# A hybrid gated-DeltaNet and dilated-attention block on one core: the key convolution's SiLU held behind the block inverse on ScalarE, and four sigmoids of a projection unit put together

## Chip, cores and metric

The kernel runs on one core of a Trainium2 chip. The metric is the device time of one execution in microseconds (us). TensorE is called PE, VectorE DVE, ScalarE ACT, GpSimd POOL, and SyncE SP; SP issues all of this kernel's DMAs.

## What is computed

One layer: the input x (1024 tokens, 1024 columns) is normalised and projected to 11280 columns; a gated delta rule over 8 heads and a dilated window attention over 12 heads run on parts of the projection; sigmoid gates (`g_a`, `g_b`) merge the two branches; an output projection, a residual and a last norm follow. What the change touches:

```python
qkv = jax.nn.silu(_causal_conv(concat([q_a, k_a, v_a]), conv_w))     # 4 taps per channel
q_a, k_a, v_a = split(qkv)
o_a = _gated_delta_rule(l2norm(q_a), l2norm(k_a), v_a, beta, g)      # chunks of 64 tokens
merged = jax.nn.sigmoid(g_a) * y_a + jax.nn.sigmoid(g_b) * y_b
```

In the delta rule each chunk of 64 tokens solves a unit lower triangular system `m u = rhs`, and a state of 128x128 is handed from chunk to chunk.

## The kernel before

**Projections.** The large products run as units of two blocks of 128 columns each. A unit (`gemm_steps`, L199) has seven products of 12 matmuls with 512 columns each, after a scheme that saves an eighth of the multiplications; each product goes to one of the PSUM banks `p_ga`, `p_gb`, `p_gc`. For each product ACT makes the high part `wh` of a weight tile (L140) and DVE the low part `wl` (L142). ACT copies the two results of bank `p_ga` out (L207 and L219), DVE adds the others (L210, L223 and L131). The third product of a unit (operand A12) writes `p_ga` again, so PE waits there until L207 has read the first.

**The delta rule.** It lies between the projection units. A half head (512 tokens, four blocks of 128) is one round, and there are 16 rounds of nearly equal length. For a round the kernel runs: the convolutions of k, q and v (`conv`: ACT scales by the first weight at L950, DVE adds three taps at L953, ACT applies SiLU at L956); `dn_prep`, which transposes k and q on PE (L1000), squares and sums them on ACT (L1003, each with a read of the accumulator), scales k into `kd`, the decay matrix into `am` and v into `vp` on ACT (all L966), and inverts blocks of 16 on DVE with a chain of small steps (L1051, L1053); `dn_run`, which doubles the inverses from 16 to 32 to 64 to 128 (L1084 to L1127) and then walks the four blocks (L1138 to L1163). The last doubling is: PE product at L1120, ACT copy to `Wv` at L1122, PE product at L1126, ACT copy into `XT` at L1127. These steps belong to different half heads: while one round's inverse is doubled, a later round's k is convolved.

**The gates.** `gate_pair` makes a projection unit whose two blocks are gate columns. Each block has two halves of 512 tokens; when a half is finished, ACT applies the sigmoid in place (L762) and SP stores it to HBM (L763). The results lie in tiles `d4`, of which there are five. Two such units (columns 0 to 511 of `g_b`) follow directly on the first head's q, k, v and z units, where the delta rule begins; the others come at the end of the delta rule.

**What sets the order.** PE runs in the order in which the program is written: every unit is a generator, and tables of positions (`CONV`, `INVERSE`, `LEVELS` and the like) say after which matmul of which unit the next step of each generator is emitted. On ACT, DVE, POOL and SP a scheduler chooses the order when the program is built, from the dependences and its own estimate of the times; `tc.issue_after(i)` adds that an instruction is to stand behind instruction `i` on its engine. `behind(last_kd)` in `conv` is such a rule: the SiLU stands behind the four `kd` instructions last written down. At run time every engine works strictly through its own list. ACT has one set of function tables active; where the next function is not in it, an ACT_TABLE_LOAD stands ahead of it. SiLU and sigmoid lie in different sets, copy and square are in each.

The change touches `gate_pair` (L750 to L765), the list of units (L872), `conv` (L947 to L957), its callers (L974, L977, L979), and L1127.

Of the kernel before, what the change touches and what calls it, by code (L numbers as in the profile page):

```python
# [11 lines left out]
AF = mybir.ActivationFunctionType  # L12
# [19 lines left out]
def hybrid_block(ctx: ExitStack, tc: tile.TileContext, x, norm_w, w_in, conv_w, a_log, dt_bias,  # L32
                 dn_norm_w, w_o_dn, w_o_dil, w_out, final_norm_w, out):
    nc = tc.nc
    V, A, G, T = nc.vector, nc.scalar, nc.gpsimd, nc.tensor
# [8 lines left out]
    def pst(tag, bufs=1):  # L44
        return ps.tile([128, 512], F32, name="p_" + tag, tag=tag, bufs=bufs)
# [9 lines left out]
    def d4():  # L55
        return dp.tile([128, 1028], F32, name="d4", tag="d4")
# [394 lines left out]
    def cw(tap, blk):  # L451
        return colp[:, tap * 24 + blk:tap * 24 + blk + 1]
# [86 lines left out]
    sg_d = {n: [dr.tile([128, S], F32, name=f"s{n}{i}") for i in range(8)] for n in ("a", "b")}  # L539
# [191 lines left out]
    def dn_unit(h, pair, t):  # L731
        def dest(n):
            o = 0 if n == "z" else 3

            def f(hf):
                if n not in t:
                    t[n] = d4()
                    if n != "z":
                        V.memset(t[n][:, 0:3], 0.0)
                return t[n][:, o + hf * 512:o + (hf + 1) * 512], idv  # L740
            return f

        def z_after(hf):
            v = t["z"][:, hf * 512:(hf + 1) * 512]
            A.activation(v, v, AF.Silu)
            nc.sync.dma_start(zsp_d[h][:, hf * 512:(hf + 1) * 512], v)

        return [(OFF[n + "a"] + h * 128, dest(n), z_after if n == "z" else nop) for n in pair]

    def gate_pair(n, i):  # L750
        bl = []
        for e in range(2):
            s = []

            def dest(hf, s=s):
                if not s:
                    s.append(d4())
                return s[0][:, hf * 512:(hf + 1) * 512], idv

            def af(hf, s=s, n=n, j=i + e):  # L760
                v = s[0][:, hf * 512:(hf + 1) * 512]
                A.activation(v, v, AF.Sigmoid)  # L762
                nc.sync.dma_start(sg_d[n][j][:, hf * 512:(hf + 1) * 512], v)  # L763
            bl.append((OFF["g" + n] + (i + e) * 128, dest, af))
        return bl  # L765

# [4 lines left out]
    def merged_at(i, hf):  # L771
        return merged[i // 4][:, hf * 4:hf * 4 + 4, i % 4]
# [34 lines left out]
    def att_head(hh, t):  # L807
        st = ap_.tile([128, 48], F32, name="st", bufs=2)
        nums = []
        return [attention(g, hh, t, st, nums) for g in range(3)] + [merge(hh, st, nums, t)]  # L810
# [51 lines left out]
    gates = [(n, i) for n in "ba" for i in range(0, 8, 2)]  # L862
    att_heads = [{} for _ in range(AH)]
    heads = [{} for _ in range(NH)]
    units = []
# [3 lines left out]
    for h in range(NH):  # L869
        units += [dn_unit(h, "qk", heads[h]), dn_unit(h, "vz", heads[h])]  # L870
        if h == 0:
            units += [gate_pair(*g) for g in gates[:2]]  # L872
    units += [gate_pair(*g) for g in gates[2:GATES]]
    units += [gate_pair(*g) for g in gates[GATES:]]
    units = [(b, w2, hops) for b in units]
    aops = {}
# [31 lines left out]
    for hh in range(AH):  # L908
        g0, g1, g2, m = att_head(hh, att_heads[hh])
# [28 lines left out]
    def full(t):  # L938
        return t[:, :16384].rearrange("c (i j) -> i c j", j=128)


    last_sub, last_wv, last_xt, last_kd = [None], [None], [None], [None]

    def behind(i):
        return tc.issue_after(i[0].ins) if i[0] else nullcontext()

    def conv(dst, u, blk, hf, late):  # L947
        o = hf * 512
        vw = (lambda a: a.rearrange("p (c t) -> p c t", t=128)) if len(dst.shape) == 3 else idv
        A.activation(dst, vw(u[:, o:o + 512]), AF.Copy, scale=cw(0, blk))  # L950
        for tap in range(1, 4):
            with behind(late):
                V.scalar_tensor_tensor(dst, vw(u[:, o + tap:o + tap + 512]), cw(tap, blk), dst, OP.mult, OP.add)  # L953
            if tap == 3:
                with behind(last_kd):
                    A.activation(dst, dst, AF.Silu)  # L956
            yield  # L957

# [12 lines left out]
    def dn_conv(h, hf, t, o):  # L971
        c0 = hf * 4
        qk = o["qk"] = dnp.tile([128, 4, 2, 128], F32, name="qk", bufs=3)
        yield from conv(qk[:, :, 0], t["k"], 8 + h, hf, last_xt)  # L974

    def qv_conv(h, hf, t, o):
        yield from conv(o["qk"][:, :, 1], t["q"], h, hf, last_sub)  # L977
        vT = o["vT"] = dnp.tile([128, 512], F32, name="vT")
        yield from conv(vT, t["v"], 16 + h, hf, last_sub)  # L979

    def dn_prep(h, hf, o):
        c0 = hf * 4
# [80 lines left out]
    def dn_run(h, hf, o, state):  # L1063
        c0 = hf * 4
        qk, am, aq, kd, vp, ce = (o[n] for n in ("qk", "am", "aq", "kd", "vp", "ce"))
        qd = qk[:, :, 1]
        X = dnp.tile([128, 4, 128], F32, name="X")
        XT = dnp.tile([128, 4, 128], F32, name="XT")
        i = nc.sync.dma_start(XT, full(inv_d[hf][1]))
# [11 lines left out]
        def prod64(lhs, rhs):  # L1081
            p = pst("ch", 2)
            for c in range(4):
                T.matmul(p[:, c * 64:(c + 1) * 64], lhs[:, c], rhs[:, c], start=True, stop=True)  # L1084
            return p
# [4 lines left out]
        pxt = prod64(X, Wv)  # L1090
# [8 lines left out]
        for c in range(4):  # L1099
            for i in range(2):  # L1100
                r, q = slice(i * 64, i * 64 + 32), slice(i * 64 + 32, i * 64 + 64)
# [11 lines left out]
        for v, p, q in ((XT, 0, 32), (XT, 64, 96), (X, 32, 0)):  # L1113
            A.activation(v[p:p + 32, :, q:q + 32], px[p:p + 32, :128].rearrange("p (c m) -> p c m", c=4), AF.Copy,
                         scale=-1.0)
# [8 lines left out]
        pxt = pst("ch", 2)  # L1124
        for c in range(4):
            T.matmul(pxt[:64, c * 64:(c + 1) * 64], X[:64, c, :64], W[:, c], start=True, stop=True)  # L1126
        A.activation(XT[:64, :, 64:], pxt[:64, :256].rearrange("p (c m) -> p c m", c=4), AF.Copy, scale=-1.0)  # L1127


        po = pst("o")  # L1130
# [73 lines left out]
    for n in range(2 * NH):  # L1204
        h, hf = n // 2, n % 2
        state = state if hf else [None]
        o = {}
        add_stream(dn_conv(h, hf, heads[h], o), steps(spread(n - 1, CONV, 4)))
        add_stream(qv_conv(h, hf, heads[h], o), steps(spread(n - 1, QV_CONV, 7)))
        add_stream(dn_prep(h, hf, o), steps([n + p for p in PREP] + spread(n, INVERSE, 16)))  # L1210
        add_stream(dn_run(h, hf, o, state), steps([n + LOAD] + spread(n + 1, LEVELS, 7) + spread(n + 1, CHAIN, 12)))
        add_stream(dn_out(h, hf, o), steps([n + 1 + p for p in OUT]))
# [168 lines left out]
    for k in range(4):  # L1381
        t = d4()[:, :S]
# [12 lines left out]
    for i in range(8):  # L1395
# [7 lines left out]
        for hf in range(2):  # L1403
            v, mv = sg[:, hs[hf]], merged_at(i, hf)
# [23 lines left out]
    for i in (0, 2, 4, 6):  # L1428
# [57 lines left out]
        with band(-1) if i == 0 else nullcontext():  # L1486
            gemm_unit(oops, lambda cb, kf, i=i: merged[kf][:, i + cb], 8,
                      lambda cb, hf, y=y: (y[cb][:, hs[hf]], idv), normed, residual if last else None, i == 0, stores, sums=V,
# [29 lines left out]
```

## Time and profile before

| | |
|---|---|
| median of 3 runs | 1437.64 us (1436.38 to 1439.87) |
| the profiled execution | 1437.49 us, of which the span from the first to the last instruction is 1435.8 us |
| mean granted clock of PE | 0.992 |
| busy: PE, DVE, ACT, POOL | 1387.7, 1076.0, 726.0, 438.7 us |
| table loads on ACT | 25 |

A row of a timeline holds the start in us from the span's start, the length in us, the engine, the line, the operation, the tile written and read, and in brackets the idle time before it and the instruction that ended it. Neighbouring rows of one kind are merged (x4). Lengths of PE rows overlap, as matmuls are pipelined.

### The profile page before, as it was taken

The page shows a single profiled execution, that of the slowest core. Times are in us where ns is not written, and L with a number is a line of the kernel's source. Part 1 is how long each engine was busy: PE and PEld are TensorE (multiplying, and loading weights), DVE is VectorE, ACT ScalarE, POOL GpSimd, SP SyncE. Part 2 cuts the span into 40 slices and gives each one's busy share as a digit, 9 for nine tenths or more (in the row PEclk, how much of TensorE's full clock was granted, in tenths as well). Part 3 has the DMA queues.
Part 4 walks back from the last instruction along what each step waited for, and adds up shares of the span by engine and source line. Part 5 has one row for each costly group of instructions (what it writes and reads, how often), then busy time and mean ns, then how long its engine had stood idle before and what let it go on. Part 6 is the DMA issues. An engine that isn't in the chain of part 4 may idle for free.

```text
span 1435.8 us, 22591 instructions
## 1 busy us (share of the span) xinstructions
PE 1387.7 (97%) x7627; PEld 1128.1 (79%) x7627; DVE 1076.0 (75%) x2305; ACT 726.0 (51%) x1830; POOL 438.7 (31%) x411
## 2 busy tenths in 40 slices
PE   7999999999999999899999999999999999999997
PEld 4788888888888888677777777777777777787786
DVE  6865567558558558778888888888887558888976
ACT  5444534534443444756555655656566436424433
POOL 6122232232323223233333333333333122431022
PEclk9999999999999999999999999999999999999999
DMA  6012333242334225533333333333334359669631
GB/s 194 24 50 67 92 101 106 67 120 87 87 83 114 75 58 135 169 84 107 98 107 100 108 113 113 99 99 106 99 107 122 111 159 296 207 219 341 215 117 59
DMA packets 228536, 172.84 MB, mean 120 GB/s; under 512 B 48802, under 2 KB 190531, under 8 KB 228420
## 3 DMA queue, kind: packets, MB, share of 16 engines
q1 hardware_dynamic: 228420, 171.40, 40.3%
q8 instruction: 60, 0.98, 0.3%
q14 instruction: 56, 0.46, 0.1%
HBM read 127.10 MB, written 44.25 MB: 119 GB/s over the span
## 4 chain that ended last, share of the span: by engine, by line
PE 78%; DVE 13%; DMA 3%; ACT 3%; issue 2%; POOL 1%; SPq 0%; POOLq 0%; DVEq 0%; ACTq 0%
PE p_gb L199 24%; PE p_ga L199 17%; PE p_gc L199 16%; DVE qk L953 5%; PE p_o L624 2%; PE p_ch L601 2%; DVE wl L142 2%; PE p_ch L1084 2%; PE p_w L1017 2%; PE p_ch L1147 1%; PE p_w L614 1%; DMA sg<-oA 1%; PE p_ch L1154 1%; PE p_o L1163 1%; PE p_ch L1126 1%
## 5 line engine op out<-in xcount | busy, mean ns | idle before, releaser
L140 ACT ACTIVATE wh<-raw 128x512 fp32r<-128x512 f32 x283 | 177.4, 628 | 276.1 <-PE p_gc L199 102.1
L142 DVE TENSOR_TENSOR wl<-raw,wh 128x512 fp32r<-128x512 f32 x283 | 208.6, 737 | 40.1 <-ACT wh L140 17.2
L174 POOL TENSOR_TENSOR raw<-raw,t 128x512 f32<-128x512 f32 x46 | 68.0, 1478 | 167.6 <-DVE wl L142 159.4
L171 POOL TENSOR_TENSOR raw<-raw,t 128x512 f32<-128x512 f32 x46 | 62.5, 1359 | 181.6 <-DVE wl L142 141.6
L953 DVE SCALAR_TENSOR_TENSOR qk<-d,colp,qk 128x512 f32<-128x512 f32 x96 | 112.1, 1169 | 1.0
L156 POOL TENSOR_TENSOR raw<-raw 128x512 f32<-128x512 f32 x47 | 72.3, 1538 | 106.9 <-DMA raw<-in_w_in_dram 57.3
L131 DVE TENSOR_TENSOR d<-p_gc,d 128x512 f32<-128x512 f32 x86 | 59.3, 690 | 41.6 <-PE p_gc L199 41.6
L199 PE MATMUL p_ga<-A12H,wh 128*128 128x512 f32 x200 | 84.9, 425 | 3.8 <-ACT d L207 3.8
L1144 POOL COPY gate<-rh 128x1 f32<-128x1 f32 x16 | 14.0, 874 | 243.1 <-DVE rh L1140 243.1
L607 ACT ACTIVATE sm<-sm,st 128x128 f32<-128x128 f32 (+1 forms) x96 | 43.1, 449 | 87.1 <-DVE st L605 87.0
L199 PE MATMUL p_gc<-S4H,wh 128*128 128x512 f32 x204 | 81.6, 402 | 1.9 <-DVE d L131 1.9
L199 PE MATMUL p_gb<-A22H,wh 128*128 128x512 f32 x204 | 82.5, 407 | 0.5 <-DVE d L210 0.5
L199 PE MATMUL p_ga<-A12L,wh 128*128 128x512 f32 x200 | 82.1, 411 | 0.0
L199 PE MATMUL p_gb<-A22L,wh 128*128 128x512 f32 x204 | 80.6, 397 | 0.0
L199 PE MATMUL p_gb<-S3H,wh 128*128 128x512 f32 x188 | 78.5, 420 | 1.9 <-DVE d L210 1.9
L199 PE MATMUL p_gc<-S4L,wh 128*128 128x512 f32 x204 | 80.2, 395 | 0.0
L199 PE MATMUL p_ga<-A11H,wh 128*128 128x512 f32 x184 | 79.5, 432 | 0.6 <-DVE gl L519 0.6
L199 PE MATMUL p_gb<-S2H,wh 128*128 128x512 f32 x188 | 79.3, 424 | 0.0
L199 PE MATMUL p_gc<-S1H,wh 128*128 128x512 f32 x188 | 78.7, 420 | 0.0
L199 PE MATMUL p_gb<-S3L,wh 128*128 128x512 f32 x188 | 76.4, 408 | 0.0
L199 PE MATMUL p_gb<-S2L,wh 128*128 128x512 f32 x188 | 76.3, 408 | 0.0
L199 PE MATMUL p_gc<-S1L,wh 128*128 128x512 f32 x188 | 75.6, 404 | 0.0
(591 smaller groups left out, 3938.7 us busy)
## 6 DMA issues: line engine op xcount, KB each, us to landing
raw<-in_w_in_dram SPq DMA_DIRECT2D x176, 256.0 KB, 2.9
wb<-w_d SPq DMA_DIRECT2D x24, 256.0 KB, 3.7
dr<-gcr_d SPq DMA_DIRECT2D x32, 128.0 KB, 3.0
dec<-de SPq DMA_DIRECT2D x32, 128.0 KB, 1.8
decq<-dr SPq DMA_DIRECT2D x32, 128.0 KB, 1.8
zsp<-d SPq DMA_DIRECT2D x16, 256.0 KB, 2.6
sb<-d SPq DMA_DIRECT2D x16, 256.0 KB, 3.3
R<-egcr_d SPq DMA_DIRECT2D x16, 256.0 KB, 3.5
```

Of the source, the lines that this page charges most:

```text
L131: last_add[0] = V.tensor_tensor(dst, vw(banks[bank]), dst, OP.add)
L140: A.activation(wh[:, :kh], v, AF.Copy)
L142: i = eng.tensor_tensor(wl[:, :kh], v, wh[:, :kh].bitcast(F32), OP.subtract)
L156: e.tensor_tensor(b12, b22, b12, OP.subtract)
L171: i = (lead["eng"] if lead else G).tensor_tensor(b11, b22, t2, OP.subtract)
L174: (sums or G).tensor_tensor(b21, b21, t2, OP.subtract)
L199: T.matmul(pt, w[:, k], m, start=new and n == 0, stop=n == len(prods) - 1, skip_group_check=not new)
L601: T.matmul(pk[:, :n], q[:, m * 128:(m + 1) * 128], k[:, (m + 1) * 128 - n:(m + 1) * 128], start=True, stop=True)
L607: last_exp[0] = A.activation(sm[:, :n], sm[:, :n], AF.Exp, scale=-1.0, bias=st[:, c_m:c_m + 1], accum_out=st[:, c_d:c_d + 1])
L624: T.matmul(po[:, j * 128:(j + 1) * 128], vt[:, m + 1 - n // 128 + i], pT[:, i * 128:(i + 1) * 128], start=i == 0, stop=i == n // 128 - 1)
L953: V.scalar_tensor_tensor(dst, vw(u[:, o + tap:o + tap + 512]), cw(tap, blk), dst, OP.mult, OP.add)
L1017: T.matmul(pk[:, j * 256:(j + 1) * 256], qk[:, c, 0], qk[:, c].rearrange("p s t -> p (s t)"), start=True, stop=True)
```

## The change

The SiLU of k is held behind the copy into `XT` that ends the last doubling (`last_inv`, L1127) instead of behind the `kd` instructions; those of q and v are held as before. In the first two gate units the four halves wait for one another: when the last is finished, four sigmoids stand in a row, the last-made half first, each followed by its store. Every other gate unit is as before.

```diff
-    def gate_pair(n, i):
-        bl = []
+    def gate_pair(n, i, together=False):
+        bl, parts = [], []
...
             def af(hf, s=s, n=n, j=i + e):
-                v = s[0][:, hf * 512:(hf + 1) * 512]
-                A.activation(v, v, AF.Sigmoid)
-                nc.sync.dma_start(sg_d[n][j][:, hf * 512:(hf + 1) * 512], v)
+                parts.append((s[0][:, hf * 512:(hf + 1) * 512], sg_d[n][j][:, hf * 512:(hf + 1) * 512]))
+
+                if not together or len(parts) == 4:
+                    first = None
+                    for v, d in parts[::-1]:
+                        with tc.issue_after(first.ins) if first else nullcontext():
+                            i = A.activation(v, v, AF.Sigmoid)
+                        first = first or i
+                        nc.sync.dma_start(d, v)
+                    parts.clear()
...
-            units += [gate_pair(*g) for g in gates[:2]]
+            units += [gate_pair(*g, together=True) for g in gates[:2]]
...
-    def conv(dst, u, blk, hf, late):
+    def conv(dst, u, blk, hf, late, silu):
...
             if tap == 3:
-                with behind(last_kd):
+                with behind(silu):
                     A.activation(dst, dst, AF.Silu)
...
-        yield from conv(qk[:, :, 0], t["k"], 8 + h, hf, last_xt)
+        yield from conv(qk[:, :, 0], t["k"], 8 + h, hf, last_xt, last_inv)
...
-        yield from conv(o["qk"][:, :, 1], t["q"], h, hf, last_sub)
+        yield from conv(o["qk"][:, :, 1], t["q"], h, hf, last_sub, last_kd)
...
-        yield from conv(vT, t["v"], 16 + h, hf, last_sub)
+        yield from conv(vT, t["v"], 16 + h, hf, last_sub, last_kd)
...
-        A.activation(XT[:64, :, 64:], pxt[:64, :256].rearrange("p (c m) -> p c m", c=4), AF.Copy, scale=-1.0)
+        last_inv[0] = A.activation(XT[:64, :, 64:], pxt[:64, :256].rearrange("p (c m) -> p c m", c=4), AF.Copy, scale=-1.0)
```

PE's order is the same instruction for instruction; only ACT's, DVE's, POOL's and SP's lists differ. The number of table loads falls from 25 to 21. From L957 on, the changed kernel's lines are those of before plus seven (L956 is L963, L1122 is L1129); L762 is L767, and L763 is L769.

ACT's list before, in the fourth round (X is the inverse so far, `jk` takes the squares, `qk` is the SiLU of k, `wh` a weight part):

```order
L1114 ACTIVATE XT<-p_ch 32x4x32 x2
L1114 ACTIVATE X<-p_ch 32x4x32
L1003 ACTIVATE jk,ssq<-p_w 128x128 x2
L956 ACTIVATE qk<-qk 128x4x128
L1003 ACTIVATE jk,ssq<-p_w 128x128
L1122 ACTIVATE Wv<-p_ch 64x256
L1003 ACTIVATE jk,ssq<-p_w 128x128
L140 ACTIVATE wh<-raw 128x512
L1127 ACTIVATE XT<-p_ch 64x4x64
L966 ACTIVATE vp<-p_w,sm 128x128 x4
```

The same place in the changed kernel:

```order
L1121 ACTIVATE XT<-p_ch 32x4x32 x2
L1121 ACTIVATE X<-p_ch 32x4x32
L1010 ACTIVATE jk,ssq<-p_w 128x128 x4
L1129 ACTIVATE Wv<-p_ch 64x256
L140 ACTIVATE wh<-raw 128x512
L1134 ACTIVATE XT<-p_ch 64x4x64
L963 ACTIVATE qk<-qk 128x4x128
L973 ACTIVATE vp<-p_w,sm 128x128 x4
```

The SiLU moved from ahead of `Wv` to behind `XT`; all four squares now stand ahead of `Wv`. The same holds in all 13 rounds from the second to the fourteenth; in the first round the SiLU stood ahead of all four squares and moved likewise; the last two rounds have no SiLU of k.

ACT's list before, where the delta rule begins (d_5460 and d_5489 are the two blocks of the first gate unit, d_5698 is the next unit's first block):

```order
L1003 ACTIVATE jk,ssq<-p_w 128x128 x2
L762 ACT_TABLE_LOAD
L762 ACTIVATE d_5460<-d_5460 128x512
L956 ACT_TABLE_LOAD
L956 ACTIVATE vT<-vT 128x512
L1003 ACTIVATE jk,ssq<-p_w 128x128
L762 ACT_TABLE_LOAD
L762 ACTIVATE d_5489<-d_5489 128x512
L1003 ACTIVATE jk,ssq<-p_w 128x128
L966 ACTIVATE kd<-p_w,eglc 128x128 x4
L966 ACTIVATE am<-am,sm 128x128 x4
L207 ACTIVATE d_5698<-p_ga 128x512
```

The same place in the changed kernel:

```order
L1010 ACTIVATE jk,ssq<-p_w 128x128 x2
L973 ACTIVATE kd<-p_w,eglc 128x128 x3
L963 ACTIVATE vT<-vT 128x512
L973 ACTIVATE kd<-p_w,eglc 128x128
L140 ACTIVATE wh<-raw 128x512
L767 ACT_TABLE_LOAD
L767 ACTIVATE d_5489<-d_5489 128x512
L767 ACTIVATE d_5460<-d_5460 128x512
L767 ACTIVATE d_5489<-d_5489 128x512
L767 ACTIVATE d_5460<-d_5460 128x512
L973 ACTIVATE am<-am,sm 128x128 x4
L207 ACTIVATE d_5698<-p_ga 128x512
```

One table load instead of three stands ahead of `am` in this stretch, and four sigmoids instead of two.

DVE's list before at the same place (`ssq` and `sm` are the small steps from the squares to the factor of `am`; L953 on d_5094 are taps of k):

```order
L142 TENSOR_TENSOR wl<-raw,wh 128x512
L953 SCALAR_TENSOR_TENSOR qk<-d_5094,colp,qk 128x4x128 x2
L1010 TENSOR_SCALAR ssq<-ssq 128x4
L1024 TENSOR_TENSOR sm<-sm,beta 128x4
L1025 TENSOR_TENSOR sm<-sm 128x4
L1026 SCALAR_TENSOR_TENSOR sm<-sm,egc 128x4
L210 TENSOR_TENSOR d_5735<-p_gb,d_5698 128x512
```

The same place in the changed kernel (`ssq` stands six rows above the first one shown):

```order
L1031 TENSOR_TENSOR sm<-sm,beta 128x4
L960 SCALAR_TENSOR_TENSOR qk<-d_5094,colp,qk 128x4x128
L1028 TENSOR_TENSOR am<-p_w,am 128x256
L1028 TENSOR_TENSOR aq<-p_w,aq 128x256
L1032 TENSOR_TENSOR sm<-sm 128x4
L142 TENSOR_TENSOR wl<-raw,wh 128x512
L1033 SCALAR_TENSOR_TENSOR sm<-sm,egc 128x4
L960 SCALAR_TENSOR_TENSOR qk<-d_5094,colp,qk 128x4x128 x2
L142 TENSOR_TENSOR wl<-raw,wh 128x512
L210 TENSOR_TENSOR d_5735<-p_gb,d_5698 128x512
```

The small steps moved ahead of the pair of taps. Since d_5460 and d_5489 are held longer, the next blocks take other buffers of the five: d_5698 takes that of d_5094, so its L207 waits for the last of these taps, and d_5735 takes that of d_5489, so its L210 waits until both stores of d_5489 have landed (before, L207 waited for the first store of d_5460, long landed).

## Rows read from the trace of the kernel before

**Rows 1.** The page, part 1: busy us, share of span, instructions.

```profile
PE 1387.7 (97%) x7627; PEld 1128.1 (79%) x7627; DVE 1076.0 (75%) x2305; ACT 726.0 (51%) x1830; POOL 438.7 (31%) x411
```

**Rows 2.** Waits of PE, whole span: us in total, times, longest us.

```profile
PE p_ch L1126 <- ACT Wv L1122: 12.3, 13, 1.0
PE p_ga L199 <- ACT d L207: 3.8, 1, 3.8
```

**Rows 3.** Timeline of ACT in the fourth round.

```profile
737.41 0.27 ACT L1114 ACTIVATE X<-p_ch 32x128 f32<-32x128 f32 x1
...
739.31 0.63 ACT L956 ACTIVATE qk<-qk 128x512 f32<-128x512 f32 x1 [0.83 <-DVE qk L953]
...
740.10 0.36 ACT L1122 ACTIVATE Wv<-p_ch 64x256 f32<-64x256 f32 x1
...
741.81 1.14 ACT L966 ACTIVATE vp<-p_w,sm 128x128 f32<-128x128 f32 x4 [0.21 <-PE p_w L1181]
```

**Rows 4.** Timeline of DVE in the fourth round: two taps of k.

```profile
735.93 3.34 DVE L953 SCALAR_TENSOR_TENSOR qk<-d,colp,qk 128x512 f32<-128x512 f32 x2
```

**Rows 5.** Timeline of PE in the fourth round: the product behind `Wv`.

```profile
740.51 0.68 PE L1126 MATMUL p_ch<-Wv,X 64*64 64x64 f32 x8 [0.94 <-ACT Wv L1122]
```

**Rows 6.** Timeline of ACT in the fifteenth round, which has no SiLU of k.

```profile
1110.11 0.27 ACT L1114 ACTIVATE X<-p_ch 32x128 f32<-32x128 f32 x1
...
1111.87 0.36 ACT L1122 ACTIVATE Wv<-p_ch 64x256 f32<-64x256 f32 x1
...
1113.59 1.14 ACT L966 ACTIVATE vp<-p_w,sm 128x128 f32<-128x128 f32 x4 [0.21 <-PE p_w L1181]
```

**Rows 7.** Timeline of PE in the fifteenth round: the product behind `Wv`.

```profile
1112.29 0.68 PE L1126 MATMUL p_ch<-Wv,X 64*64 64x64 f32 x8
```

**Rows 8.** Windows: stretch and length in us, PE busy, granted clock, DMA share, GB/s.

```profile
591.70:596.90 5.20, 5.18 (x14) 0.50 0.46 110
800.00:812.00 12.00, 11.06 (x100) 0.86 0.30 92
868.00:880.00 12.00, 11.05 (x101) 0.87 0.30 88
572.50:577.50 5.00, 3.81 (x17) 1.00 1.03 311
```

**Rows 9.** Timeline of ACT where the delta rule begins.

```profile
584.54 1.28 ACT L762 ACT_TABLE_LOAD   x1
585.84 0.64 ACT L762 ACTIVATE d<-d 128x512 f32<-128x512 f32 x1
...
589.91 1.28 ACT L966 ACTIVATE am<-am,sm 128x128 f32<-128x128 f32 x4 [2.15 <-DVE sm L1025]
591.09 0.57 ACT L207 ACTIVATE d<-p_ga 128x512 f32<-128x512 f32 x1
```

**Rows 10.** Timeline of PE there: the product that waits for L207.

```profile
591.72 0.79 PE L199 MATMUL p_ga<-A12H,wh 128*128 128x512 f32 x1 [3.78 <-ACT d L207]
```

**Rows 11.** Timeline of DVE and POOL there.

```profile
583.91 0.74 DVE L953 SCALAR_TENSOR_TENSOR qk<-d,colp,qk 128x512 f32<-128x512 f32 x1
...
585.85 2.44 DVE L953 SCALAR_TENSOR_TENSOR qk<-d,colp,qk 128x512 f32<-128x512 f32 x2
586.00 1.73 POOL L174 TENSOR_TENSOR raw<-raw,t 128x512 f32<-128x512 f32 x1 [3.38 <-DVE wl L142]
...
588.44 1.04 POOL L260 TENSOR_TENSOR sm<-ssq,neghalf 128x4 f32<-128x4 f32 x1 [0.71 <-DVE ssq L1010]
```

**Rows 12.** Timeline of DVE, ACT and PE at the end of the second gate unit.

```profile
611.07 0.67 DVE L131 TENSOR_TENSOR d<-p_gc,d 128x512 f32<-128x512 f32 x1
...
612.84 0.58 ACT L207 ACTIVATE d<-p_ga 128x512 f32<-128x512 f32 x1
...
613.75 0.39 PE L199 MATMUL p_ga<-A12H,wh 128*128 128x512 f32 x1
```

**Rows 13.** Transfers that write or read the stored gates of branch b.

```profile
DMA to landing us min/median/max: 2.0/3.6/9.2
```

More of the change, by code (lines that the diff above doesn't have):

```diff
@@ L939, in full @@
         return t[:, :16384].rearrange("c (i j) -> i c j", j=128)
-    last_sub, last_wv, last_xt, last_kd = [None], [None], [None], [None]
+    last_sub, last_wv, last_xt, last_inv, last_kd = [None], [None], [None], [None], [None]
     def behind(i):
         return tc.issue_after(i[0].ins) if i[0] else nullcontext()
-    def conv(dst, u, blk, hf, late):
+    def conv(dst, u, blk, hf, late, silu):
         o = hf * 512
```

## The prediction

> **What bounds the kernel now.** I read the page's busy times first: PE is busy for 97% of the span [rows 1], in an order that the change leaves alone, so a gain can only come from places where PE stands still or runs at the lower clock. The list of PE's waits names them. One wait has a total of 12.3 us in 13 pieces: the product at L1126 waits for ACT's copy to `Wv` [rows 2], 0.95 us each. Once the delta rule has begun, the longest single wait is 3.8 us, for the copy L207 [rows 2]. Both are waits for ACT, which is busy half of the time [rows 1]: it is not short of time, its list is in the wrong order there.
>
> The timelines show why. In a round ACT finishes X at 737.68, runs two squares, and then stands for 0.83 us at the SiLU of k, which needs DVE's third tap [rows 3]; DVE's last two taps took 3.34 us [rows 4], where one alone takes 0.74 [rows 11], and end at 739.27. SiLU and a third square follow, and `Wv` is read only at 740.10 [rows 3], so PE starts L1126 at 740.51 after 0.94 us of idling [rows 5]: 2.83 us after the end of X. The fifteenth round has no SiLU of k and shows the list that the change makes: X ends at 1110.38, four squares, `Wv` at 1111.87 [rows 6], L1126 at 1112.29 with no wait noted [rows 7]: 1.91 us after X. There the matmuls ahead of L1126, not `Wv`, set its start.
>
> Where the delta rule begins, ACT goes back and forth between sigmoid and SiLU. The squares, and with them DVE's small steps and the factor of `am`, come late: ACT waits 2.15 us for L1025, runs four `am`, and only then L207 at 591.09 [rows 9]; PE stands from 587.94 to 591.72 [rows 10]. It then works at the lower of its two clock levels (granted clock 0.50, 1.2 of 2.4 GHz) until 596.9 [rows 8]. The clock also fell in two rounds shortly after the wait at L1126 (mean 0.86 and 0.87 over 12 us) [rows 8].
>
> **The change, part by part.**
>
> *SiLU behind `XT`.* Thirteen rounds go from 2.83 to 1.91 us: 13 x 0.92 = 12.0 us, all of it on the path, as PE has nothing else to do in those gaps. In the first round the SiLU needs no waiting, and there the change puts two more squares in its place: four squares take 1.49 us from X to `Wv` [rows 6], against 0.63 for the SiLU [rows 3] and half of 1.49 for two squares: 0.1 us lost. The SiLU itself is covered in its new place: k is first used in the following round. Ends: 0 if another wait takes over (first rival), 12.3, the whole wait [rows 2].
>
> *Clock in the rounds.* A mean of 0.86 and 0.87 over 12 us means 12 x 0.14 + 12 x 0.13 = 3.2 us of lost PE time [rows 8]. Only some of thirteen like gaps were followed by such a fall, so the fall hangs on a gap that goes. I take all 3.2; ends 0 and 3.2.
>
> *Where the delta rule begins.* Four of 25 table loads go, 1.28 us each [rows 9]; their 5.1 us on ACT count only through L207. In the changed kernel two chains end at it. On ACT: everything ahead of the load at 584.54 was delayed by earlier loads that are gone, so the one that is left starts there at the latest, and a good 1 us earlier at best, once the unit's last sum is made; load 1.30, four sigmoids at about 0.53 apart (ACT rows overlap by 0.1) 2.2, four `am` 1.2: L207 at 588.1 to 589.2. On DVE: L207 now needs the last tap of k, since its block takes that buffer. That pair ended at 588.29 [rows 11]. With the small steps ahead of it, it starts about 0.2 later, and POOL's L174 beside it; whether one or both taps are stretched by it (2.44 or 3.34 for the pair [rows 11, 4]) is open: 588.4 to 589.2. So PE starts at 589.1 to 589.9, since L207 needs 0.6 [rows 9]; I take 589.5, 2.2 us earlier than 591.72. The wait for L1025 vanishes: POOL's part of that chain (L260, 1.04) started at 588.44 behind L174 and the taps [rows 11], now it stands ahead of both. An earlier gap, where PE waits for k's first SiLU, gives nothing: the next product needs q's SiLU, which now stands behind two squares.
>
> The price of the load has a second source. In the row the sigmoid starts 1.30 us after its table load did [rows 9]. The Trainium skill, page "ScalarE: Activation LUTs", section "What ACT_TABLE_LOAD costs", puts 1283 ns for the load, as here, but about 2.66 us for a switch with its drain. By that the load ahead of the sigmoids would hold L207 until 589.5 to 590.6, and this term would be an estimated 1.0 instead of 2.2 us, the whole sum 1.2 us smaller. The row has no room for a drain, so I keep 2.2.
>
> *Clock there.* 5.2 us at half speed lost 2.6 us [rows 8]. The gap that stays is 1.6 us. A gap of 1.2 us in the stretch from 572.5 to 577.5 left the clock at 1.00, gaps of 0.95 in two rounds did not [rows 8]. I take the middle, 1.3; ends 0 and 2.6.
>
> *The second gate unit.* Its last sum starts at 611.07 and the next unit's L207 at 612.84; PE takes up A12 at 613.75 without a wait [rows 12]. Four sigmoids in a row behind that sum would put L207 at 0.67 + 0.05 + 4 x 0.53 + 0.1 = 2.9 us after its start, at 614.0, and cost PE 0.8 us. But that sum, which DVE reached late, now stands seven small DVE steps further up: 0. Ends: 0.8 lost, 0.
>
> *Stores.* The same eight transfers in four and four. L210 now waits for two of them, as DVE does behind it; the later one is issued behind the third sigmoid, at 586.3 to 587.4, and landed after 3.6 us (median) [rows 13], at 591 at the latest. PE needs the result some 2.6 us after 589.5 (that work took 5.2 us at half speed [rows 8]), at 592.1, and L210 takes 0.7: covered. With a landing of 9.2 us, the longest [rows 13], it would cost 4 to 5 us.
>
> **Sum.** 12.0 - 0.1 + 3.2 + 2.2 + 1.3 = 18.6 us, against the profiled execution's 1437.5: 1418.9 us. The median, 1437.64, is 0.15 above that execution, which changes nothing. The largest terms together, with the whole clock returned, give 12.2 + 3.2 + 2.6 + 2.6 = 20.6, or 1416.9; runs lie up to 1.3 us below their median, so the low end is 1415. With 0.6 instead of 0.92 us a round (7.8), 1.2 at the beginning and no clock back it is 9.0, or 1428.5; I end the range at 1427.
>
> **The rivals.**
>
> 1. *The wait moves to `vp`.* The SiLU now stands ahead of the four `vp`. They start 1.30 us after L1126 with and without a SiLU ahead of `Wv`, with 0.21 us of waiting for PE in that [rows 3, 5 to 7]; 0.63 us of SiLU makes them 0.3 to 0.4 late against PE. If the walk over the blocks waits for them in every round, 13 x 0.35 = 4.6 us come back: 1423.5. For it: `vp` starts late already, behind a wait for PE. Against: the first block needs only the first of the four, a quarter of 1.14 us.
>
> 2. *The clock does not return.* The falls may come from the small matmuls around the gaps as much as from the gaps. Then 12.0 - 0.1 + 2.2 = 14.1: 1423.4.
>
> 3. *The change does not do what it says.* If L1126 were bound by the product ahead of `Wv` and not by ACT's list, nothing would come from the rounds, and at most 4 us from the beginning: 1434 or more. The fifteenth round speaks against it [rows 6, 7].
>
> 4. *Slower.* DVE stands at L210 until the stores of d_5489 land, and every weight part behind it stands too. A landing is free up to about 4.5 us and costs a microsecond for each one beyond that. To eat up the 15 us of the rounds and still be 0.3% slower it would have to take about 24 us, more than twice the longest seen [rows 13].
>
> **Chances.** Forecast as summed 0.64, rival 1 0.15, rival 2 0.15, rival 3 0.04, rival 4 0.02. The first three lie below 1433.2, that is faster by more than 0.3% (about what a measurement of this kernel can tell from no change): 0.94. Rival 3 is within 0.3%: 0.04. Rival 4 is slower: 0.02. Below 1415 and above 1427 I see 2 in 10 in all.
>
> **What would show it.** Right: PE's wait for `Wv` gone or down to 0.1 us a round, rounds 0.9 us shorter, the clock at 1.00 through all rounds, 21 table loads, PE's long gap at the beginning between 1.1 and 2.0 us. Wrong: a new wait of PE at L1147 (L1154 in the changed kernel) for `vp`, or at A12 for L207 in both gate units; L210 ended by a DMA; a `Wv` that starts later than 1.5 us after X.

## The result, and the profile after

The changed kernel takes **1421.18 us** (median of 4 runs, 1420.01 to 1422.61) against 1437.92 for the kernel before in the same comparison (4 runs, 1436.38 to 1439.87): a ratio of **0.9884, 95% interval 0.9869 to 0.9900**. The forecast was 1418.9 with a range of 1415 to 1427. The profiled execution took 1420.91 us; its span is 1419.2.

Line numbers are those of the changed kernel from here on (L1126 is L1133, L1122 L1129, L956 L963, L953 L960, L1147 L1154); kernels of the experiments that add lines lie a few further.

The page, part 1, of the changed kernel (busy us, share of span, instructions), beside [rows 1]: PE has the same 7627 matmuls and is busy 4.8 us less.

```profile
PE 1382.9 (97%) x7627; PEld 1123.8 (79%) x7627; DVE 1077.0 (76%) x2305; ACT 720.9 (51%) x1826; POOL 440.5 (31%) x411
```

The list of PE's waits of the changed kernel (us in total, times, longest us). The wait for `Wv` [rows 2], 12.3 us, is not in it any more. The one for L207 went from 3.8 to 1.9 us, and the one for the sum L210 has a piece of 1.9 us, which is new.

```profile
PE p_ch L1154 <- DVE rh L1147: 4.1, 14, 0.3
PE p_gb L199 <- DVE d L210: 3.8, 5, 1.9
...
PE p_ga L199 <- ACT d L207: 1.9, 2, 1.6
```

**A round.** ACT's timeline in the fourth round of the changed kernel, beside [rows 3]. X ends at 733.94, the four squares follow at once, and `Wv` starts 1.49 us after X, as in the fifteenth round of before [rows 6]. The SiLU stands behind `XT` without a wait, and `vp` behind it starts 3.42 us after X.

```profile
733.67 0.27 ACT L1121 ACTIVATE X<-p_ch 32x128 f32<-32x128 f32 x1
...
735.43 0.36 ACT L1129 ACTIVATE Wv<-p_ch 64x256 f32<-64x256 f32 x1
...
736.56 0.38 ACT L1134 ACTIVATE XT<-p_ch 64x256 f32<-64x256 f32 x1 [0.24 <-PE p_ch L1133]
736.84 0.62 ACT L963 ACTIVATE qk<-qk 128x512 f32<-128x512 f32 x1
737.36 1.11 ACT L973 ACTIVATE vp<-p_w,sm 128x128 f32<-128x128 f32 x4
```

PE's timeline there, beside [rows 5]: L1133 starts 1.91 us after X with no wait noted, on the heels of the matmul ahead of it.

```profile
735.43 0.40 PE L199 MATMUL p_gb<-S2H,wl 128*128 128x512 f32 x1
735.85 0.68 PE L1133 MATMUL p_ch<-Wv,X 64*64 64x64 f32 x8
```

**The clock.** Windows of the changed kernel (stretch and length, busy us of PE, PEld, DVE, ACT and POOL, granted clock, DMA share, GB/s), beside [rows 8]: the start of the delta rule behind PE's gap, and one of the two rounds whose clock had fallen. Both, as the other round (863 to 875), stand at 1.00, the upper level of 2.4 GHz.

```profile
590.20:595.40 5.20, 5.20 (x25) 4.28 (x26) 2.28 (x3) 5.17 (x16) 2.96 (x3) 1.00 0.46 118
796.40:808.40 12.00, 11.70 (x109) 8.97 (x109) 10.75 (x29) 8.22 (x28) 3.01 (x2) 1.00 0.45 133
```

**Where the delta rule begins.** ACT's timeline of the changed kernel, beside [rows 9]: one table load, the sigmoid 1.29 us after it, four sigmoids in 2.19 us, `am`, and L207, which waits 0.55 us for DVE's taps of k.

```profile
584.32 1.28 ACT L767 ACT_TABLE_LOAD   x1
585.61 2.19 ACT L767 ACTIVATE d<-d 128x512 f32<-128x512 f32 x4
587.71 1.27 ACT L973 ACTIVATE am<-am,sm 128x128 f32<-128x128 f32 x4
589.53 0.60 ACT L207 ACTIVATE d<-p_ga 128x512 f32<-128x512 f32 x1 [0.55 <-DVE qk L960]
```

DVE's and POOL's timeline there, beside [rows 11]: the pair of taps, with POOL's L174 beside it.

```profile
587.01 2.42 DVE L960 SCALAR_TENSOR_TENSOR qk<-d,colp,qk 128x512 f32<-128x512 f32 x2
...
587.09 1.80 POOL L174 TENSOR_TENSOR raw<-raw,t 128x512 f32<-128x512 f32 x1 [2.70 <-DVE wl L142]
```

PE's timeline of the changed kernel, beside [rows 10, 12]: A12 of the unit where the delta rule begins, and A12 and S3H (the operand of the product behind it) a unit later.

```profile
590.18 0.50 PE L199 MATMUL p_ga<-A12H,wh 128*128 128x512 f32 x1 [1.59 <-ACT d L207]
...
610.29 0.50 PE L199 MATMUL p_ga<-A12H,wh 128*128 128x512 f32 x1 [0.28 <-ACT d L207]
...
615.26 0.47 PE L199 MATMUL p_gb<-S3H,wh 128*128 128x512 f32 x1 [1.93 <-DVE d L210]
```

**The account.** PE's order is the same, so the start of each of the 7627 products can be set against the same product of before, and the difference is a running account (below 0 is earlier). It stands at +1.03 us before the delta rule (an execution's own start, in a stretch that no kernel here changes: in the profiles of the experiments it lay from -1.7 to -0.5 us). Where the delta rule begins it goes to -3.90, of that 2.6 up to A12 (2.2 of them are the wait itself, 3.78 before and 1.59 now, the rest came in small steps ahead of it) and 2.3 while PE works at the upper clock level where it had the lower. In the second gate unit it goes **back** to -2.03, 0.6 of that at A12 and 1.3 at S3H, and the first round takes 0.10. The thirteen rounds bring it to -16.14: 13 x 0.94 = 12.2 and 2.0 at the two places where the clock had fallen. The last stretch, which the change leaves alone, brings about 0.5.

| term | forecast | by the traces |
|---|---|---|
| thirteen rounds | 12.0 | 12.2 |
| first round | -0.1 | -0.1 |
| clock in the rounds | 3.2 | 2.0 |
| start, idle time | 2.2 | 2.6 |
| start, clock | 1.3 | 2.3 |
| second gate unit | 0 | -1.9 |
| sum | 18.6 | 17.1 |
| the execution's own start and end | not counted | -0.5 |

17.1 - 0.5 = 16.6 us, which is the difference of the spans, 1435.8 - 1419.2.

**Where the 1.9 us went.** DVE's timeline of the changed kernel at the end of the second gate unit: the sum L210 stands behind five taps of q and v and a weight part, and DVE is without a pause between these rows.

```profile
610.52 0.73 DVE L960 SCALAR_TENSOR_TENSOR qk<-d,colp,qk 128x512 f32<-128x512 f32 x1
...
613.77 0.73 DVE L960 SCALAR_TENSOR_TENSOR vT<-d,colp,vT 128x512 f32<-128x512 f32 x1
614.45 0.67 DVE L210 TENSOR_TENSOR d<-p_gb,d 128x512 f32<-128x512 f32 x1
```

DVE and PE in the kernel before, at the same place: there too L210 came last, and PE waited 0.66 us.

```profile
616.57 0.67 DVE L210 TENSOR_TENSOR d<-p_gb,d 128x512 f32<-128x512 f32 x1
...
617.29 0.50 PE L199 MATMUL p_gb<-S3H,wh 128*128 128x512 f32 x1 [0.66 <-DVE d L210]
```

PE comes there 3.3 us earlier (its gap begins at 613.33 and not at 616.63), the sum only 2.12. DVE's list ahead of it is the chain of small steps of the first inverse, which needs `ab`, loaded by SP. In the changed kernel DVE waits for that load:

```profile
597.21 0.17 DVE L1058 TENSOR_TENSOR tp<-ab,xb 32x15 f32<-32x15 f32 x1 [1.74 <-DMA ab<-blk]
```

In the kernel before it does not: there the chain starts at 598.93, right behind a weight part. SP's timeline of the changed kernel: the store that `ab` is read from is issued at 589.00, but the load only at 594.11, since a load of `R` now stands ahead of it and waits for POOL until 593.69.

```profile
589.00 0.37 SPq L1036 DMA_DIRECT2D blk<-am  x1
...
593.69 0.33 SPq L992 DMA_DIRECT2D R<-egcr_d  x1
594.11 0.38 SPq L1050 DMA_DIRECT2D ab<-blk  x1
```

SP's timeline of the kernel before: the store 2.21 us later, and the load 0.60 us earlier.

```profile
591.21 0.37 SPq L1029 DMA_DIRECT2D blk<-am  x1
593.51 0.33 SPq L1043 DMA_DIRECT2D ab<-blk  x1
```

### The profile page after: what moved, and what is told of

It reads as the page before. It is cut to its first block, busy times and chain, and to the rows that moved or that the text cites. A ratio compares the mean times of both kernels' runs of the same rounds, so it can differ in the third digit from the quotient of the medians.

```text
span 1419.2 us, 22571 instructions
## 1 busy us (share of the span) xinstructions
PE 1382.9 (97%) x7627; PEld 1123.8 (79%) x7627; DVE 1077.0 (76%) x2305; ACT 720.9 (51%) x1826; POOL 440.5 (31%) x411
## 4 chain that ended last, share of the span: by engine, by line
PE 82%; DVE 11%; issue 2%; DMA 2%; ACT 1%; POOL 0%; SPq 0%; POOLq 0%; DVEq 0%; ACTq 0%
PE p_gb L199 27%; PE p_ga L199 17%; PE p_gc L199 16%; PE p_o L624 2%; PE p_ch L601 2%; PE p_ch L1091 2%; PE p_w L1024 2%; DVE wl L142 2%; DVE qk L960 1%; PE p_ch L1154 1%; PE p_w L614 1%; PE p_w L1007 1%; PE p_ch L1161 1%; PE p_o L1170 1%; PE p_ch L1133 1%
## 5 line engine op out<-in xcount | busy, mean ns | idle before, releaser
L174 POOL TENSOR_TENSOR raw<-raw,t 128x512 f32<-128x512 f32 x46 | 70.0, 1522 | 167.0 <-DVE wl L142 158.8
L960 DVE SCALAR_TENSOR_TENSOR qk<-d,colp,qk 128x512 f32<-128x512 f32 x96 | 112.1, 1169 | 1.0
```

Of the source, the lines that this page charges most:

```text
L174: (sums or G).tensor_tensor(b21, b21, t2, OP.subtract)
```

## The experiments

In all kernels PE's order is that of before. The theory is the account above: the rounds' gap was ACT's list, the clock in the rounds fell because of that gap, and the second gate unit gives time back through DVE's and SP's lists. The rivals: the falls of the clock have another cause; the two halves of the change need one another; the copy to `Wv` has room. Ratios are to the kernel before, run beside each.

**1. The SiLU alone** (gate units as before).

```diff
-            units += [gate_pair(*g, together=True) for g in gates[:2]]
+            units += [gate_pair(*g) for g in gates[:2]]
```

> The SiLU of k held behind the copy into XT, all gate units as before. Theory (the two halves of the change are worth their sum, and the rounds hold most of it): 13 rounds shorter by 0.94 us, PE's wait for Wv gone, the clock at 1.00 through the rounds, the start of the delta rule as before with its wait of 3.8 us for L207: 1437.6 - 12.2 - 2.2 + 0.1 = 1423.3 us, 1 us either way. Rival (the falls of the clock in the rounds do not hang on the gap at the copy to Wv): two falls or so stay in the rounds, 1425.5. Second rival (the rounds gain only because the earlier start puts DVE and POOL ahead): the wait for Wv stays in part, 1428 or more.

Measured: 1421.7 us, ratio 0.9897 (0.9879 to 0.9916); 1423.3 against 1437.6 would be 0.9901. PE waits for `Wv` nowhere, and the wait at the start is back:

```profile
PE p_ga L199 <- ACT d L207: 3.8, 1, 3.8
```

The clock is at 1.00 in every round. So the SiLU's place is worth all that the change gains, as near as the times can tell, and both rivals fall.

**2. The gates alone** (the SiLU of k behind `kd`).

```diff
-        yield from conv(qk[:, :, 0], t["k"], 8 + h, hf, last_xt, last_inv)
+        yield from conv(qk[:, :, 0], t["k"], 8 + h, hf, last_xt, last_kd)
```

> Four sigmoids together in the first two gate units, the SiLU of k behind kd as before. Theory: 4.9 us gained where the delta rule begins, 1.9 given back in the second gate unit, and from there every round as before with 0.95 us of waiting for Wv and, in a few rounds, half the clock for some us: 1437.6 - 3.0 = 1434.6 us. Rival (what the start gains is swallowed whole by the next waits): 1437.6. If the falls of the clock hang on the gaps at Wv, at least one round of the second to fourteenth shows a granted clock under 0.95 here; if not, none need.

Measured: 1436.24 us, ratio 1.0001 (0.9986 to 1.0015). The account gains 5.1 us at the start and gives 3.4 back: 0.6 at A12, 1.3 as the wait for L210 and 1.6 by the clock, which fell behind that wait (0.79 over the 8 us from 613.1); the wait for `Wv` is as it was (12.3 us in 13 pieces). The rest went into the clock too, which in this profile fell in four rounds where the profile of before has two. Three of the windows:

```profile
942.00:946.00 4.00, 4.00 (x16) 3.41 (x16) 2.40 (x5) 1.56 (x6) 0.00 (x0) 0.57 0.35 127
1010.00:1014.00 4.00, 4.00 (x19) 3.34 (x17) 2.08 (x4) 1.86 (x6) 0.00 (x0) 0.57 0.44 153
1078.00:1082.00 4.00, 4.00 (x19) 3.52 (x20) 1.96 (x6) 2.21 (x8) 0.00 (x0) 0.58 0.45 161
```

The expected 3.0 us, a ratio of 0.9979, lie outside the interval. By the times this half of the change cannot be told from nothing; by the profile it is worth 1.7 us up to the first round, and two falls more than in the profile of before cost 2.7. The runs scatter too: the 29 executions of the kernel before and of this one, which have the gaps, range from 1432.6 to 1441.5 us (granted clock 0.997 in the shortest of this kernel, 0.989 in the longest); the six of the SiLU alone from 1420.0 to 1422.7. Over all runs of this document the standard deviation among executions of one kernel in one comparison is 2.3 us with the gaps and 1.4 without, so the gaps are only a part of the scatter.

**3. Only the first gate unit together.**

```diff
-            units += [gate_pair(*g, together=True) for g in gates[:2]]
+            units += [gate_pair(*g, together=(g is gates[0])) for g in gates[:2]]
```

> The whole change, but of the two gate units only the first has its four sigmoids together. DVE's list differs too: the sum L210 of the next unit stands behind four taps in place of five and a weight part. Theory (the 1.9 us given back in the second unit are DVE's: L210 stands behind the taps of q and v): one tap and one weight part less, about 1.1 us, and no wait of A12 for L207, 0.3: PE's wait for L210 falls from 1.9 to 0.8 us, 1421.2 - 1.4 = 1419.8. Rival (the sum comes at the same time whatever stands ahead, as PE only arrives earlier): 1421.2, with the wait of 1.9 us as it was.

Measured: 1417.74 us, ratio 0.9871 (0.9853 to 0.9889). PE's timeline: the wait at S3H is 0.86 us, and A12's is gone, as the theory said.

```profile
612.13 0.50 PE L199 MATMUL p_gb<-S3H,wh 128*128 128x512 f32 x1 [0.86 <-DVE d L210]
```

**4. The sum ahead of the taps** (`last_mid` is the last sum L210 written down; `blk` 0 and 16 are q and v of the first head, `hf` 1 is its second half).

```diff
-            with behind(late):
+            with behind(late), behind(last_mid if hf == 1 and blk in (0, 16) and tap > 1 else [None]):
                 V.scalar_tensor_tensor(dst, ...)
```

> The whole change, and in the first head's second half the last two taps of q and of v held behind the sum L210 of the unit in which they lie. The sum then stands behind two taps in place of five; its tile takes over the block whose stores the second gate unit issues first. Theory (DVE's list holds the sum): the sum starts when the matmuls ahead of it are done, PE's wait of 1.9 us is gone or under 0.3, 1421.2 - 1.7 = 1419.5. Rival (the sum then waits for those two stores to land, issued at about 608.1 and 609): a landing within 3.6 us costs nothing, one of 6 us or more brings the wait back to 1.9 us or above, 1421 to 1424, and DVE's row of the sum is ended by a DMA.

Measured: 1416.93 us, ratio 0.9873 (0.9853 to 0.9893). DVE reaches the sum at 610.87 and PE goes through without a wait; the landing of the stores plays no part:

```profile
609.59 0.73 DVE L960 SCALAR_TENSOR_TENSOR vT<-d,colp,vT 128x512 f32<-128x512 f32 x1
...
610.87 0.67 DVE L210 TENSOR_TENSOR d<-p_gb,d 128x512 f32<-128x512 f32 x1
...
611.68 0.47 PE L199 MATMUL p_gb<-S3H,wh 128*128 128x512 f32 x1
```

So the 1.9 us were held by DVE's list, with the gates untouched: by the account the second gate unit now gains 0.1 us, as the 0.6 at A12 stays and the old wait of 0.66 at S3H goes too.

**5. The changed kernel again**, beside experiments 6 to 8.

> The changed kernel once more, for the chip of this comparison: 0.9884 of the time of the kernel before, as the first time; 4.9 us gained where the delta rule begins, 1.9 given back at L210 in the second gate unit, no fall of the clock in the rounds.

Measured: 1419.15 us, ratio 0.9884 (0.9864 to 0.9904), with 1.57 us of waiting at A12, 1.96 at S3H, and no fall of the clock in the rounds.

**6. The SiLU right behind `Wv`.** Only ACT's list differs.

```diff
-        A.activation(W, pw[:64, :256].rearrange("p (c m) -> p c m", c=4), AF.Copy)
+        last_inv[0] = A.activation(W, pw[:64, :256].rearrange("p (c m) -> p c m", c=4), AF.Copy)
...
-        last_inv[0] = A.activation(XT[:64, :, 64:], ...)
+        A.activation(XT[:64, :, 64:], ...)
```

> As the changed kernel, but the SiLU of k is held behind the copy to Wv in place of the copy into XT, one instruction place or two earlier; no other engine's list differs. Theory (all that counts is that nothing stands ahead of Wv; the copy into XT comes about 0.3 us later, and the walk over the blocks has 1 us of room for that): the time of the changed kernel within 0.7 us, L1133 1.91 us after X as there. Rival (the copy into XT is just as urgent): 0.3 us in each of 13 rounds comes back as a wait for XT, 4 us slower than the changed kernel.

Measured: 1419.64 us, ratio 0.9880 (0.9861 to 0.9899), 0.5 us from the kernel of 5. ACT's timeline in the fourth round, where X ends at 732.52: `XT` comes 2.79 us after X instead of 2.62, and L1133 still 1.91 us after it.

```profile
734.01 0.37 ACT L1129 ACTIVATE Wv<-p_ch 64x256 f32<-64x256 f32 x1
734.27 0.62 ACT L963 ACTIVATE qk<-qk 128x512 f32<-128x512 f32 x1
...
735.31 0.37 ACT L1134 ACTIVATE XT<-p_ch 64x256 f32<-64x256 f32 x1
```

What counts is that the SiLU is not ahead of `Wv`; whether it stands one place or three behind it does not.

**7. Both gains at the second gate unit together** (the diffs of 3 and 4).

> Both improvements of the changed kernel that gained at the second gate unit: four sigmoids together in the first gate unit alone, and the last two taps of q and v held behind the sum L210. Theory (A12's wait for L207, 0.29 us, goes too): 0.3 us less than with the sum alone, 2.2 us less than the changed kernel. Rival (DVE's list, which changes ahead of that place as well, brings another wait): not under the kernel with the sum alone.

Measured: **1415.3 us, ratio 0.9852 (0.9837 to 0.9867)**, faster than the kernel before and the changed one: 3.9 us under the kernel of 5 beside it. By the account 2.5 of them lie in the second gate unit, where this kernel gains 0.9 us and that of 5 gives 1.6 back; the rest is within what the runs of one kernel differ by (1418.30 to 1423.34 for that of 5). A12 and S3H of the second unit run without a wait.

**8. The gap made by work.** The changed kernel with two small copies on ACT ahead of `Wv`; they serve nothing and change no result (`i` is the copy into X, `last_sq` the last of the squares). The scheduler set DVE's and SP's lists in the rounds otherwise too.

```diff
+        with tc.issue_after(i.ins), tc.issue_after(last_sq[0].ins):
+            extra = A.activation(spare, ident[:, None, :].to_broadcast([128, 2, 128]), AF.Copy)
+        with tc.issue_after(extra.ins):
+            extra = A.activation(spare[:, 0], ident, AF.Copy)
+        with tc.issue_after(extra.ins):
             A.activation(W, pw[:64, :256].rearrange("p (c m) -> p c m", c=4), AF.Copy)
```

> The changed kernel with two small copies put on ACT ahead of Wv in all 16 rounds (between them the scheduler sets a weight copy): pure work, no wait for DVE, some 1.0 us in all, about the gap that the SiLU made. Theory (Wv has no room: in the changed kernel it ends 0.05 us before PE comes to L1133; and the clock falls because of the gap, whatever makes it): a wait for Wv of about 1.0 us in 15 or 16 rounds, and in two to five of them again half the clock for some us: 1421.2 + 16 + 3 = 1440 us. Rival for the clock (it was the wait of ACT for DVE, or what DVE and POOL do at that time, not PE's gap): the gaps without a fall, 1437. Rival for the gap (only waiting counted, work ahead of Wv has room): 1421 to 1425.

Measured: 1448.03 us, ratio 1.0082 (1.0066 to 1.0098), 28.9 us above the kernel of 5, where 19 were expected. PE's waits:

```profile
PE p_ch L1138 <- ACT Wv L1134: 15.6, 15, 1.1
...
PE p_ch L1118 <- ACT W L1112: 2.7, 1, 2.7
```

The windows after four of the fifteen gaps:

```profile
674.00:678.00 4.00, 4.00 (x19) 3.34 (x17) 2.36 (x5) 2.04 (x6) 0.00 (x0) 0.57 0.39 141
810.00:815.00 5.00, 4.85 (x24) 4.18 (x25) 3.18 (x10) 2.26 (x8) 0.00 (x0) 0.66 0.37 133
946.00:951.00 5.00, 4.28 (x20) 3.65 (x21) 3.42 (x12) 2.70 (x9) 0.00 (x0) 0.66 0.44 151
1084.00:1088.00 4.00, 4.00 (x15) 3.44 (x16) 2.35 (x5) 2.04 (x6) 0.00 (x0) 0.59 0.34 124
```

The gap came as expected, 1.04 us a round, all of it on the path, and so did the falls. I had set the cost of the clock at 3 us; those four stretches lose 4 x 0.43 + 5 x 0.34 + 5 x 0.34 + 4 x 0.41 = 6.8 by their clock. A fifth fall, 5.1 us, follows a new wait of 2.7 us for `W`, in a round near the end where the copies made the scheduler set ACT's list otherwise. One more stands outside the rounds, behind the wait at S3H, where that of 5 has none (0.79 over the 8 us from 614.81, 1.7 us). 15.6 + 6.8 + 5.1 + 2.7 + 1.7 is 31.9, less 0.8 for waits for `rh` that went (from 4.1 to 3.3): 31.1, where the spans of the two profiled executions are 30.8 apart (1448.0 and 1417.2; this one was the longest of its four). ACT has no wait for DVE in this gap, so the rivals for the clock (a wait for DVE made the falls) and for the room of `Wv` fall.

**9. The load of `ab` ahead of `R` on SP.**

```diff
+        with behind(last_ab if h == 0 else [None]):
             nc.sync.dma_start(R.rearrange("p c t -> p (c t)"), ...)
...
-        nc.sync.dma_start(ab, diag(bd))
+        last_ab[0] = nc.sync.dma_start(ab, diag(bd))
```

> The changed kernel with one rule for SP: in the first head the load of R is held behind the load of ab. In the changed kernel that load of R stands ahead of it and waits 3.2 us for POOL, so ab is loaded at 594.11, later than in the kernel before (593.51), though the store that it reads was issued 2.2 us earlier; DVE then stands 1.74 us until 597.21. Theory (the 1.9 us given back at L210 come from this place in SP's list: DVE's chain of small steps, and with it the taps and the sum, starts late): the load at about 591.5, DVE's chain at 595.5 without a wait, the sum L210 1.7 us earlier, PE's wait there from 1.9 to about 0.2 us: 1.7 us less than the changed kernel, a ratio of 0.987 to the kernel before. Rival (DVE's sums of the unit and the taps decide, not the start of the chain): the wait stays at 1.9 us, a ratio of 0.988.

Measured: 1417.87 us, ratio 0.9872 (0.9852 to 0.9892). SP's timeline: the load is issued 2.4 us after the store (586.10) and not 5.1.

```profile
588.50 0.34 SPq L1051 DMA_DIRECT2D ab<-blk  x1
588.89 0.48 SPq L993 DMA_DIRECT2D R<-egcr_d  x1
```

PE's timeline: the wait at S3H falls from 1.93 to 0.47 us, where 0.2 was expected. DVE's chain starts at 592.46, right behind a weight part and without a wait for `ab`.

```profile
611.02 0.47 PE L199 MATMUL p_gb<-S3H,wh 128*128 128x512 f32 x1 [0.47 <-DVE d L210]
```

So SP's list was the other hand in it. How much of the 1.46 us is its own is open: the scheduler also set one weight part (0.6 us) behind the sum L210 that stood ahead of it, and no run here parts the two.

**10. The same rule in the kernel of 7.**

> The same rule for SP in the kernel that has four sigmoids together in the first gate unit alone and the sum L210 ahead of two taps each. Theory: that kernel has no wait left at L210, so the earlier load brings nothing, a ratio of 0.985 as there. Rival: DVE, now ahead, also makes the sums in the next unit earlier, and one of the small waits that follow goes: 0.984.

Measured: 1416.12 us, ratio 0.9852 (0.9827 to 0.9877), that of 7: with no wait left there, an earlier load buys nothing.

The intervals of 3, 4, 9 and of the changed kernel overlap; that each gains is read from PE's waits, not from the times. Only that of 7 (up to 0.9867) all but parts from that of the changed kernel beside it (from 0.9864); its four executions (1414.60 to 1416.32) lie under all four of that kernel (1418.30 to 1423.34).

## Why the prediction was right, and where it was off

*What bounds the kernel, and the rounds:* right. The fifteenth round [rows 6, 7] was a true picture of the others without the SiLU: 1.49 and 1.91 us, to the hundredth. "The matmuls ahead of L1126, not `Wv`, set its start" is half of it: `Wv` ends at X + 1.86 and the matmul ahead of L1133 at X + 1.89, so both set it, and experiment 8 shows that no work fits ahead of `Wv` any more. The cover of the SiLU in its new place held (experiments 1 and 6).

*The clock in the rounds:* the mechanism was right (experiments 2 and 8: falls with the gap, whatever makes it; none in the nine profiles without it), its size was not: 2.0 us, where 3.2 had been read off a mean clock [rows 8]. While the clock was low, the kernel before lost 1.5 and 1.6 us in the account, 3.1 in all, so the mean clock was read rightly; but 0.4 to 0.5 of each came back at once, as two rounds now wait for `rh` (14 times, before 12; L1154 waits 0.28 us there) which the low clock had covered. The prediction counted PE's lost time as if no wait stood behind it. The number of falls also varies between executions, so a term taken from the two in one profile was uncertain by its own size.

*Where the delta rule begins:* A12 was forecast for 589.1 to 589.9 and, with this execution 1.03 us late, came at 590.18, that is 589.2; 2.6 us instead of 2.2, though the wait itself shrank by 2.2. L207 was ended by DVE's taps, as foretold, whose pair took 2.42 us beside POOL's L174, where a single tap takes 0.73. The Trainium skill, page "SBUF — State Buffer", section "SBUF: two separate sides", says that DVE and GpSimd share one port pair and that a DVE operation with two inputs in SBUF and a GpSimd one that reads SBUF shut each other out; these rows agree.

*The table load:* as read from the row [rows 9]. The sigmoid starts 1.29 us after the load, and L207 waits for DVE, not for ACT. The Trainium skill's 2.66 us for a switch (page "ScalarE: Activation LUTs", section "What ACT_TABLE_LOAD costs") would have shown as a sigmoid at 586.98 or later; no second part is to be seen between those rows.

*Clock there:* 1.3 had been taken as the middle of 0 and 2.6; it was 2.3. With a gap of 1.6 us the clock stayed at 1.00, in each of the ten profiles that have this gap; behind the 3.8 us of experiment 1 it fell (0.79 over 8 us).

*The second gate unit:* **this step failed.** "0" was argued from L207 alone: the sum ahead of the sigmoids comes early enough. It did, nearly (PE waited 0.28 us, 0.6 in the account). But at the next product, S3H, L210 on DVE was the last to come already in the kernel before, by 0.66 us, a wait that the prediction left out; whatever PE gained ahead of it beyond what DVE gained was lost again. DVE gained only 2.12 us, as SP's list had changed as well: `R` ahead of `ab`. The prediction went through ACT's and DVE's lists here, not through SP's. Experiment 4 shows DVE's part; experiment 9 shows SP's, though not its exact size.

*Rivals:* `vp` did not become a wait (L1154 waits for `rh` by 0.3 us as before, two times more); the clock did return; the change did what it says; L210 did not wait for stores, but it was the right instruction to be wary of, for another reason.

That the sum came this close is in part luck: errors of opposite sign, +1.0 and +0.4 at the start and +0.2 in the rounds against -1.9 in the second gate unit and -1.2 for the clock in the rounds, left it 1.5 us too high, and the execution's own start and end did the rest.

## What to carry to other kernels

When a stretch of the busiest engine gets shorter, look up the next place where another engine comes last, however small that wait is: what is gained ahead of it is kept only as far as that engine's own chain gets earlier too, and that chain may run through a DMA queue whose order the scheduler has quietly changed. A round without the disputed instruction is the best forecast of all rounds without it. A wait of 1 us in a loop can cost more than its own length: here some of these gaps, not all, were followed by a stretch at the lower clock level, and 1.5 to 1.7 us were lost each time. How many it is differs between executions, and so does the time.

## What had not been expected of the hardware

The clock fell after some of the gaps of 0.94 to 1.04 us in the rounds (2 of 13, 4 of 13 and 4 of 15 in three profiles), in stretches where PE runs many small products (some 100 matmuls in 12 us [rows 8]). After the gap of 1.6 us where the delta rule begins, amid products of 512 columns, it fell in none of ten profiles; after the 1.9 us at S3H, amid such products too, in two of five (those of experiments 2 and 8). So the length of a gap alone did not tell whether the clock would fall. Which gap of thirteen it would be, no run here shows.

SP's list, which nobody meant to change, cost a share of what the gates gained: one load that waits 3.2 us for POOL held the load behind it, which was issued 0.42 us after it (594.11) and 5.1 us after the store that it reads.
